# Seven-product MLP weights: product 4 is split from product 6's raw tile after GpSimd adds a block onto it in SBUF

## The chip, the cores and the metric

The kernel runs on 1 core of one Trainium2 chip. The metric is device microseconds for one execution of the whole program. Before the change the median of three runs is 756.41 us (756.36 to 757.88).

## The reference, cut to what matters

One layer of an encoder trunk, float32 in and out, 512 tokens, width 1024, hidden width 4096:

```python
h = h + jnp.concatenate([fox_out, rec], axis=-1) @ w_out[l]
h = h + memory_cross_attention(rmsnorm(h, norm_x_g[l]), mem_n, w_xq[l], w_xkv[l], w_xo[l])
u = rmsnorm(h, norm_ff_g[l]) @ w1[l]
h = h + jnp.square(jax.nn.relu(u)) @ w2[l]
return rmsnorm(h, final_norm_g)
```

The change is in the last two products, with `w1` (1024 x 4096) and `w2` (4096 x 1024).

## The kernel before, in words

Every weight is used as a sum of two parts, `hi` and `lo`. A raw float32 tile of 128 x 1024 is loaded into SBUF; ScalarE writes `hi` from it (line 181, tiles `wh...`), VectorE writes `lo = raw - hi` (line 185, tiles `wl...`); TensorE then runs three matmuls for each product of tiles: hi x hi, hi x lo, lo x hi.

The MLP is cut into eight sets `g` of 512 hidden columns. For each set there is an up part (with `w1`) and a down part (with `w2`). Up parts of sets 2 to 7 and all down parts use a seven-product scheme for 2 x 2 blocks: instead of eight block products there are seven, called 1, 5, 6, 2, 7, 3, 4 and run in this order. Products 1, 2, 3 use a block of the weights as it is; 5, 7, 6 and 4 use sums of blocks: W5 = W00 + W01, W7 = W01 + W11, W6 = W11 + W5, W4 = W10 + W6.

Those four sums are made in DRAM ahead of time (`sum_jobs`, line 430 on). For each, SyncE starts a copy of a block into a DRAM tile `ws...` (line 434), and GpSimd later starts an accumulating DMA that adds the second addend to it (line 444). So 14 weight sets (eight down, six up) make 56 copies and 56 accumulating DMAs. `Presum` spreads the 56 over the program: a counter of matmul work (`tick`) is compared with `PACE`, pairs of a start and a gap, and each accumulating DMA is made to wait for the matmul at which it fell due. `COPIES` says how many copies go out beside each load of the earlier stages.

A unit is one weight tile of one product. `load` starts the DMA of its raw tile on SyncE's queue (line 1328), up to `LOADS` = 8 units ahead of use; `prep` emits the two splits, up to 4 units ahead, since the pools of `wh` and `wl` tiles have four buffers. Tile names are made of kind, set and product: `whu36` is the hi part for up, set 3, product 6; `wrd24` is the raw tile for down, set 2, product 4.

In the up part (`mlp_up7`) the seven products share three PSUM banks. Products 1, 6, 7 and 4 accumulate in bank U, 5 and 3 in Y, 2 in V. Behind product 6 ScalarE copies U into Y (line 1411, tile `uY`):

```python
            elif name == "6":
                ac.activation(bank["Y"], ps, AF.Copy)
```

Product 2 runs in V meanwhile; product 7 writes U again and therefore waits for that copy. TensorE's order is written by hand; ScalarE's, VectorE's, GpSimd's and SyncE's orders come from a scheduler, and each of these engines runs its own list strictly in order. An instruction that waits holds up all that stand behind it on its engine.

Of the kernel before, what the change touches and what calls it, by code (L numbers as in the profile page):

```python
# [13 lines left out]
ALU = mybir.AluOpType  # L14
# [3 lines left out]
S = 512  # L18
# [4 lines left out]
WT = 256  # L23
# [14 lines left out]
X1, X2, X3, X4 = 1.5, 2.0, 1.5, 2.0  # L38
NEG = -3.0e38
SEVEN = (2, 3, 4, 5, 6, 7)  # L40
RAWS, HB, LOADS = 6, 4, 8
COPIES = {7: 2, 16: 1, 17: 0, 21: 1, 29: 2}
PACE = (183.0, 4.6), (306.0, 6.0), (385.0, 9.0)


@with_exitstack
def emit(
# [21 lines left out]
    nc = tc.nc  # L69
    te, ve, ac, gp = nc.tensor, nc.vector, nc.scalar, nc.gpsimd  # L70
# [26 lines left out]
    def s4(shape, name, dt=F32):  # L97
        return s4p.tile([P] + shape, dt, tag="s4", name=name)
# [7 lines left out]
    def t4(name):  # L106
        return t4p.tile([P, D], F32, tag="t4", name=name)

    def t2(name, dt=F32, shape=(S,)):
        return t2p.tile([P] + list(shape), dt, tag="t2", name=name)  # L110
# [18 lines left out]
    def f(a):  # L129
        return a.bitcast(F32)  # L130
# [39 lines left out]
    UW, UK = WT + FH, KC // 2  # L170

    def new_parts(shape, name):
        pad = [P, UK * (UW + FH)]
        hi = whp.tile([P, shape[0] * shape[1]], R, tag="wh", name=f"wh{name}", padded_shape=pad)
        lo = wlp.tile([P, shape[0] * shape[1]], R, tag="wl", name=f"wl{name}", padded_shape=pad)
        return [t.rearrange("p (k n) -> p k n", k=shape[0]) for t in (hi, lo)]

    def split_of(hi, lo, raw):
        def split(what="hl"):
            if "h" in what:  # L180
                ac.activation(hi, raw, AF.Copy)  # L181
            if "v" in what:
                ve.tensor_copy(hi, raw)
            if "l" in what:
                ve.tensor_tensor(lo, raw, f(hi), ALU.subtract)  # L185

        return split

    def load_unit(name, spec, ks, parts=1, between=None):
# [12 lines left out]
        for q in range(parts):  # L202
# [3 lines left out]
            if between is not None:  # L206
                between(q)
            for _ in range(next((n for at, n in reversed(COPIES.items()) if len(stream) >= at), 0)):
                if copies:
# [78 lines left out]
    def ahead(n):  # L288

        return tc.high_priority(offset=n) if n else nullcontext()  # L290

    class Fill:
        def __init__(self):
            self.q = deque()
            self.credit = 0.0
# [115 lines left out]
    hn_hi, hn_lo = act_tile("hn_hi"), act_tile("hn_lo")  # L411
    xTd = drp.tile([4, P, 2, S], F32, name="xTd")

    SUMS = {"5": ("00", "01"), "7": ("01", "11"), "6": ("11", "5"), "4": ("10", "6")}

    def block1(g, rc):
        r, c = int(rc[0]), int(rc[1])
        n0 = g * HG + c * WT
        return w1[r * S : (r + 1) * S, n0 : n0 + WT].rearrange("(k p) n -> p k n", p=P)

    def block2(g, rc):
        r, c = int(rc[0]), int(rc[1])
        k0 = g * HG + r * 2 * P
        return w2[k0 : k0 + 2 * P, c * S : (c + 1) * S].rearrange("(k p) n -> p k n", p=P)

    wsum = {}

    def sum_jobs(kind, g):
        block, shape = (block1, [P, UK, WT]) if kind == "u" else (block2, [P, 2, S])
        for name in SUMS:  # L430
            wsum[kind, g, name] = drp.tile(shape, F32, name=f"ws{kind}{g}{name}")

        def first(name):
            dma = nc.sync.dma_start(wsum[kind, g, name], block(g, SUMS[name][0]))
            copied.add((kind, g, name))
            return dma

        def sums():
            for name, (_, b) in SUMS.items():
                while (kind, g, name) not in copied:  # L440
                    copies.popleft()()
                src = wsum[kind, g, b] if b in SUMS else block(g, b)
                more = {"max_dma_last_dim": 2048} if b in SUMS else {}
                yield gp.dma_start(wsum[kind, g, name], src, accum_op=ALU.add, **more)  # L444

        return [lambda name=name: first(name) for name in SUMS], sums()

    class Presum:
        def __init__(self):
            self.jobs, self.spent, self.next, self.at = deque(), 0.0, PACE[0][0], None  # L450

# [12 lines left out]
        def tick(self, us, at):  # L464
            self.spent, self.at = self.spent + us, at
            while self.jobs and self.spent >= self.next:
                gap = next(gap for begin, gap in reversed(PACE) if self.next >= begin)
                if gap is None:
                    self.next = min(begin for begin, _ in PACE if begin > self.next)
                    continue  # L470
# [448 lines left out]
    for c in range(NT):  # L919
# [24 lines left out]
        with ahead(P1):  # L944
            hs = sm(4, f"hs{c}")
            for h in range(4):
                j = t2(f"hj{c}{h}", F32, (P,))
# [134 lines left out]
    for n in range(len(pairs) + 2):  # L1082
        if n < len(pairs):
            p, tb = pairs[n]
# [217 lines left out]
    for i in range(2):  # L1302
        gp.dma_start(gfin[i], final_norm_g[i * S : (i + 1) * S].partition_broadcast(P))
    HS = S // 2
    units, unit_q = {}, deque()
    sqs, comb, hbs = {}, {}, {}
    PRODUCTS = ("1", "5", "6", "2", "7", "3", "4")
    QUAD = {"1": "00", "2": "10", "3": "11"}
    raw_n = [0]

    def raw_tile(name):
        raw_n[0] += 1
        if raw_n[0] % RAWS == 4:
            return t4(f"wr{name}")
        if raw_n[0] % RAWS in (0, 2):
            return wrp.tile([P, D], F32, tag="wr", name=f"wr{name}", padded_shape=[P, UK * UW])
        return s4([D], f"wr{name}")

    load_q = deque()

    def add_unit(key, shape, src):

        name = "".join(map(str, key))
        box = []

        def load():
            raw = raw_tile(name).rearrange("p (k n) -> p k n", k=shape[0])
            nc.sync.dma_start(raw, src())
            box.append(raw)

        def prep():
            while not box:
                load_q.popleft()()
            unit = new_parts(shape, name)
            with ahead(PW):
                split_of(unit[0], unit[1], box[0])()
            units[key] = unit

        unit_q.append((key, prep))
        load_q.append(load)  # L1340

    def up_units(g):
        if g in SEVEN:
            for name in PRODUCTS:
                add_unit(("u", g, name), [UK, WT], lambda name=name: block1(g, QUAD[name]) if name in QUAD else wsum["u", g, name])
            return
        for j in range(2):
            for n in range(2):
                add_unit(("u", g, j, n), [UK, WT], lambda j=j, n=n: block1(g, f"{n}{j}"))

    def down_units(gs):
        for name in PRODUCTS:
            for g in gs:
                add_unit(("d", g, name), [2, S], lambda g=g, name=name: block2(g, QUAD[name]) if name in QUAD else wsum["d", g, name])

    def unit(*key):

# [278 lines left out]
    for g in range(NG):  # L1636
        if g >= 2:
            up_units(g)
        if 1 <= g < NG - 1:
            down_units((g - 1,))  # L1640
    down_units((NG - 2, NG - 1))
    order = [k for k, _ in unit_q]
    xsum = {}
# [78 lines left out]
```

## Time and profile before

| what | value |
|---|---|
| median of 3 runs | 756.41 us |
| the profiled execution's own time | 756.48 us |
| span of its trace, first to last instruction | 754.5 us |
| VectorE busy / ScalarE busy / GpSimd busy | 71% / 57% / 25% |
| DMA moved over the span | 162.85 MB, mean 216 GB/s |
| TensorE clock granted over the span | 0.999 |
| seven-product stage | about 450 to 748 us of the span |

Times in the trace count from the span's first instruction. A row of the timeline gives the start, how long, the engine, the line, the operation and its tiles, and in brackets how long the engine stood idle before it and what released it. A row of DMA issues gives the median from the issue to the landing of the last byte. Tile names stand there without set and product numbers.

### The profile page before, as it was taken

How to read it: one execution, taken by the hardware profiler on the slowest of the kernel's cores; microseconds unless marked ns; L12 is line 12 of the kernel's file. 1: busy time of each engine (PE TensorE's matmuls, PEld its weight loads, DVE VectorE, ACT ScalarE, POOL GpSimd, SP SyncE). 2: the span in 40 equal slices, each digit the busy share in tenths (PEclk: the TensorE clock that was granted, in tenths of full speed). 3: DMA queues.
4: the chain of work that ended last, by engine and by line, in shares of the span. 5: the costliest groups of instructions: out<-in, count | busy, mean ns of one | idle time of the engine just before them, and what ended most of it. 6: DMA issues, size and time to landing. Idle time of an engine off the chain costs nothing.

```text
span 754.5 us, 12053 instructions
## 1 busy us (share of the span) xinstructions
PE 746.1 (99%) x4501; PEld 648.9 (86%) x4501; DVE 537.4 (71%) x844; ACT 431.1 (57%) x715; POOL 190.3 (25%) x274
## 2 busy tenths in 40 slices
PE   9999999999999999999999999999999999999996
PEld 6889888888888988888888888898989899999985
DVE  5647873677878756745546558978787887879697
ACT  5655555655756532334434396657575757574873
POOL 7207531333342237620121211111000111000014
PEclk9999999999999999999999999999999999999999
DMA  8641987567947899996668879898979797977332
GB/s 251 196 117 57 310 262 226 177 225 252 312 165 222 264 280 290 287 245 128 140 151 182 179 127 312 198 314 229 296 186 298 190 281 205 265 220 248 121 112 112
DMA packets 112444, 162.85 MB, mean 216 GB/s; under 512 B 6482, under 2 KB 73595, under 8 KB 112387
## 3 DMA queue, kind: packets, MB, share of 16 engines
q1 hardware_dynamic: 91186, 123.80, 49.9%
q0 software_dynamic: 20608, 37.25, 27.2%
q10 hardware_dynamic: 592, 1.05, 0.4%
q8 instruction: 35, 0.57, 0.3%
q14 instruction: 23, 0.18, 0.1%
HBM read 157.87 MB, written 62.93 MB: 293 GB/s over the span
## 4 chain that ended last, share of the span: by engine, by line
PE 95%; DVE 1%; ACT 1%; POOL 1%; issue 1%; ACTq 0%; POOLq 0%
PE U L1528 4%; PE U L1527 4%; PE U L1529 4%; PE uU L1402 3%; PE uU L1401 3%; PE uU L1400 3%; PE xq L253 2%; PE wo L253 2%; PE xq L254 2%; PE xw L253 2%; PE xq L255 2%; PE xw L255 2%; PE u L255 2%; PE xw L254 2%; PE wo L255 2%; PE u L254 2%
## 5 line engine op out<-in xcount | busy, mean ns | idle before, releaser
L185 DVE TENSOR_TENSOR wld<-wrd,whd 128x1024 fp32r<-128x1024 f32 x56 | 69.6, 1244 | 17.4 <-ACT whd L181 17.3
L181 ACT ACTIVATE whd<-wrd 128x1024 fp32r<-128x1024 f32 x56 | 59.2, 1057 | 24.6 <-PE uV L1401 8.0
L181 ACT ACTIVATE whu<-wru 128x1024 fp32r<-128x1024 f32 x42 | 44.5, 1059 | 44.9 <-PE uU L1401 18.2
L185 DVE TENSOR_TENSOR wlu<-wru,whu 128x1024 fp32r<-128x1024 f32 x42 | 50.4, 1223 | 14.5 <-ACT whu L181 14.4
L1527 PE MATMUL U<-whd,hb 128*128 128x512 f32 x120 | 46.8, 390 | 0.0
L1528 PE MATMUL U<-wld,hb 128*128 128x512 f32 x120 | 46.8, 390 | 0.0
L1529 PE MATMUL U<-whd,hb 128*128 128x512 f32 x120 | 46.7, 389 | 0.0
L444 POOL DMA_DIRECT2D wsd<-in_w_dram x16 | 16.8, 1050 | 91.5 <-PE U L1529 27.9
L444 POOL DMA_DIRECT2D wsd<-wsd x16 | 14.3, 894 | 98.4 <-PE uU L1402 18.0
L1012 POOL TENSOR_SCALAR bi<-nF,Ft 128x128 f32<-128x128 f32 (+3 forms) x32 | 20.7, 656 | 60.2 <-PE pt L1044 34.7
L444 POOL DMA_DIRECT2D wsu<-in_w_dram x12 | 14.1, 1176 | 58.8 <-PE xq L255 11.4
L1155 ACT ACTIVATE x_hi<-hT,gv 128x512 fp32r<-128x512 f32 x16 | 11.5, 717 | 27.7 <-DVE hT L1154 27.7
L1402 PE MATMUL uU<-x_hi,wlu 128*128 128x256 f32 x96 | 27.2, 283 | 0.0
L1400 PE MATMUL uY<-xs_hi,whu 128*128 128x256 f32 x96 | 27.2, 283 | 0.0
L1401 PE MATMUL uY<-xs_lo,whu 128*128 128x256 f32 x96 | 27.2, 283 | 0.0
L1402 PE MATMUL uY<-xs_hi,wlu 128*128 128x256 f32 x96 | 27.2, 283 | 0.0
L1400 PE MATMUL uU<-xs_hi,whu 128*128 128x256 f32 x96 | 27.2, 283 | 0.0
L1401 PE MATMUL uU<-xs_lo,whu 128*128 128x256 f32 x96 | 27.2, 283 | 0.0
L1402 PE MATMUL uU<-xs_hi,wlu 128*128 128x256 f32 x96 | 27.2, 283 | 0.0
L1401 PE MATMUL uU<-x_lo,whu 128*128 128x256 f32 x96 | 27.2, 283 | 0.0
L1400 PE MATMUL uU<-x_hi,whu 128*128 128x256 f32 x96 | 27.1, 283 | 0.0
L1529 PEld LDWEIGHTS U<-whd,hb 128*128 128x128 f32 x120 | 22.5, 188 | 4.7
(995 smaller groups left out, 2655.2 us busy)
## 6 DMA issues: line engine op xcount, KB each, us to landing
wsd<-in_w_dram SPq DMA_DIRECT2D x32, 512.0 KB, 5.7
wrd<-wsd SPq DMA_DIRECT2D x32, 512.0 KB, 6.3
wsu<-in_w_dram SPq DMA_DIRECT2D x24, 512.0 KB, 7.1
wrd<-in_w_dram SPq DMA_DIRECT2D x24, 512.0 KB, 6.2
wru<-wsu SPq DMA_DIRECT2D x24, 512.0 KB, 6.2
wru<-in_w_dram SPq DMA_DIRECT2D x18, 512.0 KB, 5.8
wsd<-in_w_dram POOLq DMA_DIRECT2D x16, 512.0 KB, 8.0
wsd<-wsd POOLq DMA_DIRECT2D x16, 512.0 KB, 6.8
```

Of the source, the lines that this page charges most:

```text
L181: ac.activation(hi, raw, AF.Copy)
L185: ve.tensor_tensor(lo, raw, f(hi), ALU.subtract)
L253: te.matmul(ps, wh, hi, start=n_ == 0 and not begun, stop=False)
L254: te.matmul(ps, wh, lo, start=False, stop=False)
L255: at = te.matmul(ps, wl, hi, start=False, stop=k == order[-1])
L444: yield gp.dma_start(wsum[kind, g, name], src, accum_op=ALU.add, **more)
L1400: te.matmul(ps[:, i, :], whi[:, k, ws], xh[:, k, :], start=begin, stop=False, skip_group_check=True)
L1401: te.matmul(ps[:, i, :], whi[:, k, ws], xl[:, k, :], start=False, stop=False, skip_group_check=True)
L1402: at = te.matmul(ps[:, i, :], wlo[:, k, ws], xh[:, k, :], start=False, stop=k == UK - 1, skip_group_check=True)
L1527: te.matmul(ps, hi, whi[:, k, :], start=begin, stop=False, skip_group_check=True)
L1528: te.matmul(ps, hi, wlo[:, k, :], start=False, stop=False, skip_group_check=True)
L1529: at = te.matmul(ps, lo, whi[:, k, :], start=False, stop=k == 1, skip_group_check=True)
```

## The change

The sum W4 is no longer made in DRAM: `SUMS` loses "4", and with it 14 copies (SyncE), 14 accumulating DMAs from one DRAM tile to another (GpSimd) and 14 loads (SyncE) go. In their place product 6's raw tile is kept. Once both of its splits have read it, GpSimd starts an accumulating DMA that adds the block W10 from DRAM onto that tile in SBUF, and the two splits of product 4 read the same tile. The raw tiles of product 6 now always come from the pool `s4` (12 buffers) and are held until product 4 is split; `RAWS` goes from 6 to 5, so that the other raw tiles rotate over fewer places. `PACE` spreads the 42 sums that are left; `COPIES` loses its last entry.

```diff
-RAWS, HB, LOADS = 6, 4, 8
-COPIES = {7: 2, 16: 1, 17: 0, 21: 1, 29: 2}
-PACE = (183.0, 4.6), (306.0, 6.0), (385.0, 9.0)
+RAWS, HB, LOADS = 5, 4, 8
+COPIES = {7: 2, 16: 1, 17: 0, 21: 1}
+PACE = (183.0, 5.1), (306.0, 12.5)
...
-    SUMS = {"5": ("00", "01"), "7": ("01", "11"), "6": ("11", "5"), "4": ("10", "6")}
+    SUMS = {"5": ("00", "01"), "7": ("01", "11"), "6": ("11", "5")}
...
-        if raw_n[0] % RAWS == 4:
+        if raw_n[0] % RAWS == 3:
             return t4(f"wr{name}")
...
         def load():
-            raw = raw_tile(name).rearrange("p (k n) -> p k n", k=shape[0])
-            nc.sync.dma_start(raw, src())
+            if part == "4":
+                box.append(raws.pop((kind, g)))
+                return
+            if part == "6":
+                raw = raws[kind, g] = s4(shape, f"wr{name}")
+            else:
+                raw = raw_tile(name).rearrange("p (k n) -> p k n", k=shape[0])
+            if part in SUMS:
+                src = wsum[kind, g, part]
+            else:
+                src = block(g, QUAD[part] if part in QUAD else f"{key[3]}{part}")
+            nc.sync.dma_start(raw, src)
             box.append(raw)
...
             with ahead(PW):
                 split_of(unit[0], unit[1], box[0])()
+            if part == "6":
+                gp.dma_start(box[0], block(g, "10"), accum_op=ALU.add)
             units[key] = unit
```

TensorE's list of matmuls is the same in both kernels, matmul for matmul. Two places on the other engines matter below. The first is ScalarE's list in the up part of set 3. Before:

```order
L181 ACTIVATE whu36_5522<-wru36_5433 128x1024
L181 ACTIVATE whu32_5548<-wru32_5456 128x1024
L181 ACTIVATE whu37_5582<-wru37_5479 128x1024
L1406 ACTIVATE uV3_5579<-uU3_5547 128x512
L1476 ACTIVATE hb22_5711<-sq21_5137 128x512
L181 ACTIVATE whu33_5614<-wru33_5503 128x1024
L1409 ACTIVATE y53_5612<-uY3_5581 128x512
L181 ACTIVATE whu34_5645<-wru34_5526 128x1024
L1411 ACTIVATE uY3_5581<-uU3_5547 128x512
L181 ACTIVATE whd21_5677<-wrd21_5552 128x1024
```

And now:

```order
L181 ACTIVATE whu36_5482<-wru36_5393 128x1024
L181 ACTIVATE whu32_5507<-wru32_5416 128x1024
L181 ACTIVATE whu37_5540<-wru37_5439 128x1024
L1415 ACTIVATE uV3_5537<-uU3_5506 128x512
L181 ACTIVATE whu33_5572<-wru33_5462 128x1024
L1418 ACTIVATE y53_5570<-uY3_5539 128x512
L1485 ACTIVATE hb22_5669<-sq21_5100 128x512
L181 ACTIVATE whu34_5603<-wru36_5393 128x1024
L1420 ACTIVATE uY3_5539<-uU3_5506 128x512
L181 ACTIVATE whd21_5636<-wrd21_5511 128x1024
```

The split `whu34` reads `wru36`, the raw tile that `whu36` read seven rows above, in place of a raw tile of its own; `hb22` moved down by two rows; the copy `uY3` stands right behind `whu34`, as it did.

The second place is GpSimd's list near the end of the sums, before:

```order
L444 DMA wsd67_242<-in_w2_dram 256x1x512
L444 DMA wsd77_246<-in_w2_dram 256x1x512
L444 DMA wsd66_243<-wsd65_241 256x512
L444 DMA wsd76_247<-wsd75_245 256x512
L444 DMA wsd64_244<-wsd66_243 256x512
L444 DMA wsd74_248<-wsd76_247 256x512
```

And now:

```order
L444 DMA wsd67_230<-in_w2_dram 256x1x512
L1350 DMA wru56_6202<-in_w1_dram 128x4x256
L444 DMA wsd77_233<-in_w2_dram 256x1x512
L1350 DMA wrd46_6386<-in_w2_dram 128x2x512
L444 DMA wsd66_231<-wsd65_229 256x512
L444 DMA wsd76_234<-wsd75_232 256x512
L1350 DMA wru66_6607<-in_w1_dram 128x4x256
L1350 DMA wrd56_6791<-in_w2_dram 128x2x512
```

The two sums of W4 (`wsd64`, `wsd74`) are gone, and the additions onto raw tiles (`wru56`, `wrd46`, `wru66`, `wrd56`) stand between the sums that are left: `wru56` right behind `wsd67`, `wru66` right behind `wsd76`.

More of the change, by code (lines that the diff above doesn't have):

```diff
@@ L1304, in emit @@
     HS = S // 2
-    units, unit_q = {}, deque()
+    units, raws, unit_q = {}, {}, deque()
     sqs, comb, hbs = {}, {}, {}
@@ L1319, in emit, with add_unit @@
     load_q = deque()
-    def add_unit(key, shape, src):
+    def add_unit(key, shape):
+        kind, g, part = key[:3]
         name = "".join(map(str, key))
+        block = block1 if kind == "u" else block2
         box = []
         def load():
-            raw = raw_tile(name).rearrange("p (k n) -> p k n", k=shape[0])
-            nc.sync.dma_start(raw, src())
+            if part == "4":
[10 more added lines that the diff above has]
+            nc.sync.dma_start(raw, src)
             box.append(raw)
@@ L1342, in up_units @@
     def up_units(g):
[L1343 to L1349, printed above, removed]
+        for part in PRODUCTS if g in SEVEN else [(j, n) for j in range(2) for n in range(2)]:
+            add_unit(("u", g, part) if g in SEVEN else ("u", g, *part), [UK, WT])
     def down_units(gs):
@@ L1353, in down_units @@
             for g in gs:
-                add_unit(("d", g, name), [2, S], lambda g=g, name=name: block2(g, QUAD[name]) if name in QUAD else wsum["d", g, name])
+                add_unit(("d", g, name), [2, S])
     def unit(*key):
```

## The prediction

> **What bounds the kernel now.** First the page: the span, the engines' busy time, and the chain that ended last.
>
> ```profile
> span 754.5 us, 12053 instructions
> PE 746.1 (99%) x4501; PEld 648.9 (86%) x4501; DVE 537.4 (71%) x844; ACT 431.1 (57%) x715; POOL 190.3 (25%) x274
> ...
> PE 95%; DVE 1%; ACT 1%; POOL 1%; issue 1%; ACTq 0%; POOLq 0%
> ```
>
> TensorE fills the span. Busy could still hide waits, so I asked the view of waits for TensorE alone. It has two rows:
>
> ```profile
> PE warm L365 <- DVE ones L369: 1.3, 1, 1.3
> PE pt L1044 <- DVE bi L1036: 0.7, 1, 0.7
> ```
>
> 2.0 us, neither in the MLP. The table of windows (busy time and, in brackets, instructions of PE, PEld, DVE, ACT, POOL; then granted clock, DMA share, GB/s) has TensorE full over the whole stage:
>
> ```profile
> 440.00:690.00 250.00, 250.00 (x1501) 224.29 (x1501) 203.48 (x245) 165.42 (x223) 26.93 (x30) 1.00 0.89 240
> ```
>
> So nothing that goes off DMA, GpSimd or SyncE can shorten the path; the matmuls are the same. What the change can do is make TensorE wait where it doesn't today. I looked for the instruction at which it would, in the timeline of up set 3 (the names of set and product are from the engines' lists):
>
> ```profile
> 535.02 3.50 DVE L185 TENSOR_TENSOR wlu<-wru,whu 128x1024 fp32r<-128x1024 f32 x3
> ...
> 541.47 1.06 ACT L181 ACTIVATE whu<-wru 128x1024 fp32r<-128x1024 f32 x1 [1.34 <-PE uU L1401]
> 542.44 0.58 ACT L1411 ACTIVATE uY<-uU 128x512 f32<-128x512 f32 x1
> ...
> 542.57 1.23 DVE L185 TENSOR_TENSOR wlu<-wru,whu 128x1024 fp32r<-128x1024 f32 x1 [1.66 <-ACT whu L181]
> ...
> 544.27 0.28 PE L1400 MATMUL uU<-xs_hi,whu 128*128 128x256 f32 x1
> ```
>
> The first row is three lo splits, products 6, 2 and 7; a split takes 1.22, so product 6's ends at 535.02 + 1.22 = 536.24, the last reader of raw tile 6. At 541.47 ScalarE splits product 4, then copies U into Y until 542.44 + 0.58 = 543.02. At 544.27 product 7 writes U, which waits for that copy. Today the copy is 1.25 us early.
>
> **The change part by part.** *Removed:* 14 copies, 14 sums, 14 loads. All run beside a TensorE that never waits for them: 0 us. *RAWS, COPIES, the order of loads:* raw tiles are asked for some 20 us ahead and split when a `wh` buffer comes free, not when they land; the copies and sums left start no later than they need to. 0 us; the cover is that lead.
>
> *Added:* an accumulating DMA between product 6's lo split and product 4's hi split. Split 4 stands ahead of the copy uY on ScalarE, so a late landing delays the copy, and product 7 behind it. From 536.24 to 544.27 there are 8.03 us. The split and copy take 543.02 - 541.47 = 1.55. Each hand-over between engines takes about 0.04 (lo split 4 starts at 542.57, its hi split ends at 542.53), four of them 0.16. That leaves **6.3 us** from GpSimd's issue to the landing; each microsecond over it is lost by TensorE. It waits for nothing else there, and the next cycle keeps the spacing, so losses add up over the up sets.
>
> How long does such a DMA take? The view of DMA issues over the stage 440 to 690 us, where the last row is from the whole span:
>
> ```profile
> q0 software_dynamic: 8684, 14.72, 36.4%
> ...
> wsd<-wsd POOLq DMA_DIRECT2D x9, 512.0 KB, 6.9
> wsd<-in_w_dram POOLq DMA_DIRECT2D x8, 512.0 KB, 8.0
> wsu<-wsu POOLq DMA_DIRECT2D x6, 512.0 KB, 7.5
> wsu<-in_w_dram POOLq DMA_DIRECT2D x4, 512.0 KB, 7.7
> ```
>
> ```profile
> mt<-in_mem_dram POOLq DMA_DIRECT2D x2, 512.0 KB, 4.6
> ```
>
> No row adds onto SBUF. The nearest is the last but one, the same source, size and engine with a DRAM target: 7.7. The lower end is mt, a plain GpSimd load into SBUF: 4.6. For the upper end, five of today's sums start within 1 us of such a lo split's end in sets 2 to 6:
>
> ```profile
> 496.88 0.89 POOL L444 DMA_DIRECT2D wsu<-wsu  x1 [6.06 <-PE uU L1402]
> ...
> 654.48 0.88 POOL L444 DMA_DIRECT2D wsd<-wsd  x1 [8.14 <-PE uY L1402]
> ```
>
> Asked for one by one (issues at 496.88, 536.10, 575.32, 615.25, 654.48) they landed after:
>
> ```profile
> wsu<-wsu POOLq DMA_DIRECT2D x1, 512.0 KB, 9.8
> ```
>
> ```profile
> wsd<-in_w_dram POOLq DMA_DIRECT2D x1, 512.0 KB, 9.1
> ```
>
> ```profile
> wsd<-wsd POOLq DMA_DIRECT2D x1, 512.0 KB, 6.8
> ```
>
> ```profile
> wsd<-in_w_dram POOLq DMA_DIRECT2D x1, 512.0 KB, 7.8
> ```
>
> ```profile
> wsd<-wsd POOLq DMA_DIRECT2D x1, 512.0 KB, 8.7
> ```
>
> Upper end 9.8, median 8.7. It is a crowded moment: the next parts' loads are in flight, as the DMA share, the number before the last, shows for sets 3, 6 and 7.
>
> ```profile
> 536.20:542.70 6.50, 6.50 (x56) 6.50 (x55) 4.28 (x6) 4.46 (x7) 0.94 (x1) 1.00 1.04 300
> ...
> 653.90:660.40 6.50, 6.50 (x57) 6.50 (x56) 4.28 (x6) 4.47 (x7) 0.88 (x1) 1.00 1.03 330
> 692.50:699.60 7.10, 7.10 (x62) 7.10 (x61) 3.76 (x5) 4.34 (x6) 0.00 (x0) 1.00 0.79 267
> ```
>
> I take **7.4**: 7.7 less a tenth of the way to mt, for the target in SBUF. Sets 2 to 6 then lose 7.4 - 6.3 = 1.1 each, 5.5 in all.
>
> The Trainium skill speaks against this: its page "DMA: Bandwidth & Descriptors", section "Anatomy of one DMA — SWDGE (gpsimd) path", gives 2.0 us plus bytes / 436 GB/s, by which 512 KB would land after an estimated 3.2 us; the rows (6.8 to 9.8) don't agree. By it this term would be 0.
>
> *Queued behind another sum.* All GpSimd DMAs share queue 0. In the stage its 27 issues took 36.4% of 250 us, 91 us: 3.4 us of all 16 engines each. One that follows another closer than that I count as landing 3.4 behind it. Where are the sums? In today's timeline the last sum starts at 664.55 and the sixteenth from last at 516.90; fifteen gaps of 9.0 on the counter, 135.0, took 147.65, 1.094 us per unit:
>
> ```profile
> 516.90 1.05 POOL L444 DMA_DIRECT2D wsd<-in_w_dram  x1 [4.79 <-PE U L1529]
> ...
> 664.55 0.88 POOL L444 DMA_DIRECT2D wsd<-wsd  x1 [9.20 <-PE uU L1402]
> ```
>
> Today's last falls due at 520.2 on the counter; the new pace puts its last, wsd76, at 510.5, so 664.3 - 9.7 x 1.094 = 653.7, and wsd67, three gaps of 12.5 earlier, at 612.7. The lo splits of product 6 in sets 5 and 6:
>
> ```profile
> 613.46 3.50 DVE L185 TENSOR_TENSOR wlu<-wru,whu 128x1024 fp32r<-128x1024 f32 x3
> ...
> 652.68 3.50 DVE L185 TENSOR_TENSOR wlu<-wru,whu 128x1024 fp32r<-128x1024 f32 x3
> ```
>
> They end at 614.68 and 653.90. In set 5 the addition follows wsd67 by 2.1: +1.3. In set 6 it must wait for wsd76's issue (0.9, from 653.9 to 654.8: +0.9) and follows by 0.9: +2.5. Together **4.7**.
>
> *Set 7* has no sums beside it and a wider gap:
>
> ```profile
> 691.30 2.35 DVE L185 TENSOR_TENSOR wlu<-wru,whu 128x1024 fp32r<-128x1024 f32 x2
> ...
> 701.15 0.28 PE L1400 MATMUL uU<-xs_hi,whu 128*128 128x256 f32 x1
> ```
>
> 701.15 - 692.52 = 8.63, so 6.9 are allowed; at a DMA share of 0.79 I count 0, at 8.7 it would be 1.8.
>
> *Down sets.* Lo split 6 ends at 551.21 + 1.23 = 552.44, hi split 4 starts at 561.30; 8.8 are allowed, and no PSUM copy stands right behind it. 0.
>
> ```profile
> 551.21 1.23 DVE L185 TENSOR_TENSOR wld<-wrd,whd 128x1024 fp32r<-128x1024 f32 x1 [0.28 <-ACT whd L181]
> ...
> 561.30 1.06 ACT L181 ACTIVATE whd<-wrd 128x1024 fp32r<-128x1024 f32 x1
> ```
>
> **Sum:** 5.5 + 4.7 = 10.2 on the span of 754.5; outside the span the profiled execution has 2.0 (756.48), which stays. 756.48 + 10.2 = 766.7, and against the median, 756.41, I say 766.5.
>
> **The rivals.** *It lands in time* (the other side). If the addition onto SBUF is more like mt than like the sums, below 6.3 us, the copy uY is never late in sets 2 to 5, and where queue 0 interleaves its DMAs not in 6 either. For it: DRAM is neither read nor written for the target. Against it: the DMA share of 1.04 in the very window. Time 756.5. It decides at 6.3; between 4.6 and 6.3 with strict queueing, set 6 alone loses up to 3.4 and set 5 up to 1.3, 758 to 761.
>
> *All land late.* The five same-phase sums are the measure: 8.7 - 6.3 = 2.4 in five sets, 12.0, 4.7 for the queue and 1.8 in set 7: 18.5, time 775.
>
> *The clock drops in the longest hole.* Set 6's hole is 1.1 + 3.4 = 4.5 us. If an idle TensorE gets a slower clock, it pays again afterwards. No hole of such length is in this trace; 0 by its rows, granted clock 1.00 in the windows above. The Trainium skill's "TensorE: Matmul & The Clock Gate", section "Part 1: The HAM clock gate (the "warmup" mystery)", has half the clock after an idle window of some 3.4 us, until a busy window as long; an estimate by it is 1.7 us more, 768; no run here shows it.
>
> *Raw tiles come late.* Tile 6 is held over four units more, so loads could find no place, and `wh` splits would starve at TensorE. Against it: a lead of 20 us. Price at one missed load per cycle of about 3 us, six cycles: 785.
>
> *Less DMA early shortens the first 440 us.* The most there is to win is the two waits, 2.0 us: 754.5.
>
> **How the numbers follow.** Forecast (a late uY in up sets, 758 to 772) 0.65; all late 0.13; in time 0.13; clock 0.03; raw tiles 0.02; early gain 0.04. A measurement of this kernel tells 0.2%, 1.5 us, from none. Faster 0.04; same 0.13; slower 0.83. The range reaches from "in time" to "all late": 756.5 to 775; left out are the early gain, the late raw tiles and the outer halves of those two.
>
> **What would show it.** TensorE's waits get rows for the first matmul of product 7 (uU) released by ScalarE's uY, six of them at most, the longest in set 6; ScalarE's split whu gets waits for a DMA in front of them; a row wru<-in_w_dram on POOLq near 7.4 us. In the down sets no TensorE wait. I am wrong if that row is under 6.3, if waits of TensorE name a `wh` or `wl` tile, or if time moves before 440 us.

## The result and the profile after

The changed kernel takes 789.32 us (median of 6 runs, 787.72 to 792.20), the kernel before 756.41 on the same chip (755.73 to 757.88): a ratio of 1.0437 (95% interval 1.0413 to 1.0462). The sign was forecast, the size was not: 33 us were lost in place of 10. Below, a time that is set against a trace is that execution's own span: 754.5 before, 786.2 after.

The page of the changed kernel: the span, TensorE's row (busy time, share of the span, instructions), and the chain that ended last by engine and by line.

```profile
span 786.2 us, 11996 instructions
...
PE 755.5 (96%) x4501; PEld 656.6 (84%) x4501; DVE 541.3 (69%) x844; ACT 430.4 (55%) x715; POOL 196.5 (25%) x274
...
PE 66%; issue 21%; DMA 5%; POOL 3%; DVE 2%; ACT 2%; SPq 0%; POOLq 0%; ACTq 0%; DVEq 0%
```

TensorE has gone from 99% to 96%, and DMA, which had no share of the chain, has 5%. (The 21% under "issue" are not idle TensorE: here the chain is followed back along GpSimd's list, and what lies between two of its DMAs is counted there, 13.03 us behind the sum at 503.71 for example.) But TensorE's busy time has grown too, from 746.1 to 755.5, with the same 4501 matmuls: 9.4 us that no wait explains. So there are two losses to look for. The view of waits for TensorE (total, how many, longest; a fourth row, 0.3 us, is left out), and one row of the same view for ScalarE:

```profile
PE uU L1409 <- ACT uY L1420: 21.8, 6, 5.0
PE warm L365 <- DVE ones L369: 1.3, 1, 1.3
PE pt L1044 <- DVE bi L1036: 0.7, 1, 0.7
```

```profile
ACT whu L181 <- DMA wru<-in_w_dram: 35.4, 6, 7.2
```

This is the place that was forecast: six waits of product 7 (uU) on the copy uY, and one step back six waits of ScalarE's split whu on the addition. Up set 3 shows the chain in the timeline, ScalarE first, then TensorE:

```profile
544.34 0.62 ACT L1485 ACTIVATE hb<-sq 128x512 fp32r<-128x512 f32 x1
549.99 1.06 ACT L181 ACTIVATE whu<-wru 128x1024 fp32r<-128x1024 f32 x1 [5.03 <-DMA wru<-in_w_dram]
550.95 0.58 ACT L1420 ACTIVATE uY<-uU 128x512 f32<-128x512 f32 x1
```

```profile
551.59 0.39 PE L1409 MATMUL uU<-xs_hi,whu 128*128 128x256 f32 x1 [2.85 <-ACT uY L1420]
```

ScalarE stands idle for 5.03 us in front of the late split; the copy, which itself needs nothing that is late, stands behind it; TensorE has a hole, a stretch without work, of 2.85 us. The holes of sets 2 to 7 are 2.2, 2.9, 4.3, 5.0, 4.9 and 2.5. Against the matmuls of before, no shift worth naming arises ahead of 440 us or in a down set.

How late the additions onto a raw tile land, from the view of DMA issues (KB, then median from issue to landing): first over 440 to 760 us, then the six up additions one by one, sets 2 to 7.

```profile
wrd<-in_w_dram POOLq DMA_DIRECT2D x8, 512.0 KB, 5.8
...
wru<-in_w_dram POOLq DMA_DIRECT2D x6, 512.0 KB, 9.8
```

```profile
wru<-in_w_dram POOLq DMA_DIRECT2D x1, 512.0 KB, 8.9
...
wru<-in_w_dram POOLq DMA_DIRECT2D x1, 512.0 KB, 8.2
...
wru<-in_w_dram POOLq DMA_DIRECT2D x1, 512.0 KB, 10.5
...
wru<-in_w_dram POOLq DMA_DIRECT2D x1, 512.0 KB, 11.2
...
wru<-in_w_dram POOLq DMA_DIRECT2D x1, 512.0 KB, 11.0
...
wru<-in_w_dram POOLq DMA_DIRECT2D x1, 512.0 KB, 9.1
```

The same 512 KB onto SBUF take 5.6 to 6.4 us in down sets 0 to 5 (7.3 and 10.0 in sets 6 and 7, where the second follows the first by 2.3 us) and 8.2 to 11.2 in an up set. Two things differ: the hour, and the packets, 256 of 2 KB in a down set and 512 of 1 KB in an up set. The windows during up set 3's addition, down set 2's, down set 4's and up set 7's (busy time and instructions of five engines, then granted clock, DMA share, GB/s):

```profile
541.70:549.90 8.20, 7.03 (x59) 6.83 (x57) 2.94 (x3) 2.06 (x3) 2.50 (x2) 1.00 1.03 286
560.10:565.80 5.70, 5.70 (x29) 4.74 (x28) 3.90 (x6) 4.17 (x6) 1.20 (x1) 1.00 0.67 127
...
652.50:658.90 6.40, 6.40 (x32) 5.33 (x31) 4.61 (x7) 4.69 (x7) 1.21 (x1) 1.00 1.00 234
721.90:731.00 9.10, 8.27 (x69) 8.06 (x68) 3.05 (x3) 2.64 (x4) 1.30 (x1) 1.00 0.98 244
```

The DMA share alone does not tell them apart: down set 4's addition took 6.4 us beside a share of 1.00. By the packet records SyncE's queue started 0.2 MB of loads while down set 2's addition was in flight, 0.8 beside down set 4's, and 1.3 to 2.1 beside the six up additions. e5, e6 and e7 below take queue, packets and loads one at a time.

The second loss is in the column of the granted clock, the share of full speed at which TensorE was allowed to run. Windows cut where that column changes, around the holes of sets 2 and 3, and then of set 4 (in the second fence the last row comes first in time):

```profile
505.94:509.35 3.41, 1.56 (x13) 1.57 (x14) 1.83 (x2) 3.13 (x5) 0.00 (x0) 1.00 1.01 199
509.35:512.76 3.41, 3.41 (x19) 3.41 (x18) 1.99 (x3) 2.03 (x3) 0.00 (x0) 0.50 0.56 156
546.90:550.31 3.41, 1.83 (x16) 1.63 (x14) 0.00 (x0) 0.32 (x1) 1.17 (x1) 1.00 1.06 249
550.31:553.72 3.41, 2.13 (x17) 2.14 (x18) 2.40 (x2) 3.31 (x5) 0.00 (x0) 1.00 1.13 160
553.72:557.14 3.42, 3.42 (x31) 3.42 (x30) 2.54 (x4) 2.96 (x4) 0.00 (x0) 1.00 0.54 162
```

```profile
594.68:598.09 3.41, 2.77 (x13) 2.77 (x14) 2.45 (x2) 3.23 (x6) 0.00 (x0) 0.50 0.22 47
598.09:601.50 3.41, 3.41 (x18) 3.41 (x18) 1.34 (x2) 0.94 (x2) 1.08 (x1) 0.50 0.62 140
...
591.27:594.68 3.41, 0.00 (x0) 0.00 (x0) 0.00 (x0) 0.95 (x1) 0.00 (x0) 1.00 0.59 181
```

A matmul here has 256 columns; an interval of 3.41 us filled with them has 18 or 19 at 0.50 and 31 at 1.00. Set 4's hole empties a whole interval, and two intervals at half follow; set 2's leaves 1.56 of 3.41 busy, and one follows; set 3's, though longer than set 2's, is cut in two by the border at 550.31, and none follows. In all, 20.5 us of the MLP run at half, TensorE busy in 18.2 of them.

What each loss is worth follows from the start of every matmul in the two traces. The changed kernel is 0.35 us behind ahead of the first hole, falls back at the six holes by 2.4, 3.0, 4.4, 5.2, 5.1 and 2.7, together 22.8 (0.16 more than each wait), and in between by 1.6, 0.1, 2.8, 1.6 and 2.4, together 8.4. The 0.1 of set 3, where no half clock follows, is lost at the second matmul behind the hole; the rest arises where the clock is at half. 0.35 + 22.8 + 8.4 = 31.5 of the 31.7 us by which the spans differ.

### The profile page after: what moved, and what is told of

It is laid out like the page before. It is cut to its first block, busy times and chain, and to the rows that moved or that the text cites. A ratio compares the mean times of both kernels' runs of the same rounds, so it can differ in the third digit from the quotient of the medians.

```text
span 786.2 us, 11996 instructions
## 1 busy us (share of the span) xinstructions
PE 755.5 (96%) x4501; PEld 656.6 (84%) x4501; DVE 541.3 (69%) x844; ACT 430.4 (55%) x715; POOL 196.5 (25%) x274
## 4 chain that ended last, share of the span: by engine, by line
PE 66%; issue 21%; DMA 5%; POOL 3%; DVE 2%; ACT 2%; SPq 0%; POOLq 0%; ACTq 0%; DVEq 0%
DMA wru<-in_w_dram 4%; PE wo L253 2%; PE xw L255 2%; PE xw L254 2%; PE xw L253 2%; PE u L253 2%; PE wo L254 2%; PE u L254 2%; PE u L255 2%; PE wo L255 2%; PE xq L254 2%; PE xq L255 2%; PE xq L253 2%; PE U L1537 1%; PE pv L1060 1%
## 5 line engine op out<-in xcount | busy, mean ns | idle before, releaser
L1409 PE MATMUL uU<-xs_hi,whu 128*128 128x256 f32 x96 | 31.3, 326 | 21.8 <-ACT uY L1420 21.8
L1409 PEld LDWEIGHTS uU<-xs_hi,whu 128*128 128x128 f32 x96 | 21.7, 226 | 23.0 <-ACT uY L1420 23.0
L1350 POOL DMA_DIRECT2D wrd<-in_w_dram x8 | 9.6, 1198 | 93.6 <-DVE wld L185 93.6
L1410 PE MATMUL uU<-xs_lo,whu 128*128 128x256 f32 x96 | 30.5, 317 | 0.0
L1411 PE MATMUL uU<-xs_hi,wlu 128*128 128x256 f32 x96 | 30.4, 317 | 0.0
```

The costliest lines, as they stand in the source:

```text
L1409: te.matmul(ps[:, i, :], whi[:, k, ws], xh[:, k, :], start=begin, stop=False, skip_group_check=True)
L1410: te.matmul(ps[:, i, :], whi[:, k, ws], xl[:, k, :], start=False, stop=False, skip_group_check=True)
L1411: at = te.matmul(ps[:, i, :], wlo[:, k, ws], xh[:, k, :], start=False, stop=k == UK - 1, skip_group_check=True)
```

## The experiments

The edits are made on the changed kernel. All but e3, e8, e11 and e12 are a single execution, beside before at 756.5 to 756.7. Executions of the changed kernel itself lie between 787.7 and 796.5 (e9), so a single time a few us apart decides little; waits, landings and clock in the trace do. "Landings" are those of the six up additions, sets 2 to 7.

**e1: is it what stands behind the late split?** The hi split of product 4 is put behind the copy uY on ScalarE.

```diff
-                ac.activation(hi, raw, AF.Copy)
+                made = ac.activation(hi, raw, AF.Copy)
+                if behind is not None:
+                    order_only = mybir.DependencyInfo(mybir.DependencyClass.NoSync, mybir.DependencyReason.DATA)
+                    tc.add_manual_dep(made.ins, behind.ins.name, order_only, reason="behind")
...
-                split_of(unit[0], unit[1], box[0])()
+                split_of(unit[0], unit[1], box[0])(behind=ycopy.get(g) if (kind, part) == ("u", "4") else None)
...
-                ac.activation(bank["Y"], ps, AF.Copy)
+                ycopy[g] = ac.activation(bank["Y"], ps, AF.Copy)
```

> The changed kernel, with product 4's hi split in the up parts placed one row lower on ScalarE, behind the copy uY. Theory (TensorE waits for uY because that split, which waits for the addition's landing, stands ahead of it): the six waits of uU on uY go, 21.8 us and the 10 us lost to the halved clock with them. The next late thing is then VectorE's sum sq (uU with y5), which product 4 waits for and which stands behind lo split 4, lo split d1 and an hb part: the landing + 5.6 us. Landings after 8.2 to 11.2 us make that some 8 us in sets 2 to 6, so 764 to 768, and no dip of the clock. Rival (the additions slow TensorE through DMA or SBUF traffic, or raw tiles come late): still 780 to 790.

Measured 775.96. The waits on uY are gone, and the next thing late is the one that was named, VectorE's sum sq, which stands behind product 4's lo split:

```profile
PE uU L1412 <- DVE sq L1427: 13.9, 6, 5.4
```

The place is confirmed; the time missed its range by 8, since landings (9.8, 8.3, 11.2, 9.9, 13.3, 9.6) and half clock (10.2 us of it, none expected) were both underrated again.

**e2: do holes or traffic drop the clock?** TensorE gets 20 matmuls on a spare bank ahead of product 7, so that it works through most of the hole.

```diff
+NFILL = 20
...
+            if name == "7":
+                junk = sc(f"junk{g}").rearrange("p (i n) -> p i n", i=2)
+                for n in range(NFILL):
+                    te.matmul(junk[:, 0, :], whi[:, n % UK, 0:P], xh[:, n % UK, :], start=n == 0, stop=n == NFILL - 1, skip_group_check=True)
```

> The changed kernel, with 20 filler matmuls of 256 columns into a spare PSUM bank ahead of product 7 in each up part of sets 2 to 7 (2.4 us each where the clock is full). They add nothing to the output. Theory (the trace has 21.8 us of holes, and about 10 us more because the granted clock halves after a hole): fillers run inside the holes, what is left of the waits for uY is about 8 us with none over 3 us, the clock stays at 1.0, and the time falls by about 10 us although 120 matmuls are added: 777 to 781. Rival (the slower matmuls behind the holes come from the addition's traffic, not from the idle time): the slow matmuls stay, 787 to 792.

Measured 785.58, above the theory's 781 and below the rival's 787. The holes that are left are at most 4.1 us, and half clock fell from 20.5 us to 3.4, one interval behind the longest, at a traffic that was no smaller (60.82 MB over 440 to 760 us, 60.80 in the changed kernel). So holes drop the clock, and the traffic does not. The time missed because in sets 2 to 6 the additions, issued at the same place, landed later still (9.5 to 12.6; 7.9 in set 7), so that fillers and holes together, 14.4 + 11.7 us, are more than the 21.8 us of holes that they replace.

```profile
PE uU L1414 <- ACT uY L1425: 11.7, 5, 4.1
```

**e3 and e4: down sets alone, up sets alone.** `names_of(kind)` keeps the old sum W4 for the other kind; the gap of `PACE` is set so that the sums end where the change has them.

```diff
+    def names_of(kind):
+        return [n for n in SUMS if n != "4" or kind != KEPT]
...
-            if part == "6":
+            if part == "6" and kind == KEPT:
                 gp.dma_start(box[0], block(g, "10"), accum_op=ALU.add)
```

> Only the eight down parts keep the change; in the up parts W4 is summed in DRAM and loaded as before (48 sums, gap 8.5 in place of 12.5 so that the last one falls at about the same time). Theory (all of the loss sits in the up parts): 756.0 to 757.5, no wait of TensorE in the MLP, GpSimd's additions onto wrd landing after 5.5 to 9 us. Rival (holding raw tile 6, five raw places or GpSimd's queue cost something by themselves): 759 or more.

> Only the six up parts keep the change; in the down parts W4 is summed in DRAM and loaded as before (50 sums, gap 8.0). Theory: the loss of the changed kernel is all here, 784 to 795; with more sums and more loads beside them the additions land after 8 to 12 us, and the clock dips in sets where the hole is over about 4 us. Rival (the loss is shared): 765 to 780.

Down alone: 756.98 (10 runs), ratio 1.0002 (0.9989 to 1.0015), with no wait of TensorE in the MLP. Up alone: 791.14, as long as the changed kernel itself. The whole loss is in the up sets, and eight copies, sums and loads fewer gain nothing.

**e5: the queue.** All 42 sums are over before the first addition.

```diff
-PACE = (183.0, 5.1), (306.0, 12.5)
+PACE = ((183.0, 3.9),)
```

> Only the pace of the 42 sums in DRAM changes: they come every 3.9 on the counter, so that the last starts before the first addition onto a raw tile. GpSimd's queue then carries nothing but the additions in the MLP. After: the up additions land 8.9, 8.2, 10.5, 11.2, 11.0, 9.1 us after their issue in sets 2 to 7, with packets of other sums ahead in sets 4, 5 and 6. Theory (the queue makes sets 4 to 6 longer than the others, the crowd of SyncE's loads does the rest): sets 4 to 6 fall to 8.5 to 9.5, sets 2, 3 and 7 stay within 1 us; waits of uU on uY 14 to 18 us in place of 21.8; with the half clock after the longest hole or two 771 to 781 us. Rival 1 (the queue is all of it): all six land in 6.5 or less, no waits, 757. Rival 2 (the queue is nothing): 10 to 11 in sets 4 to 6 as before, waits 20 or more, 784 to 790.

Measured 776.73, the time as the theory had it; landings 8.4, 8.2, 8.2, 8.2, 7.9, 10.6. Sets 4 to 6 land 2.3 to 3.1 us earlier, somewhat more than expected, sets 2 and 3 0.5 and 0.0. Set 7, with no sums in either kernel, became 1.5 longer, which the theory did not have: by the packet records 1.9 MB of SyncE's loads were started while it was in flight, 1.0 to 1.3 in the others. That the loads are the cause is not shown by this run alone.

```profile
PE uU L1409 <- ACT uY L1420: 13.9, 6, 3.8
```

```profile
wru<-in_w_dram POOLq DMA_DIRECT2D x6, 512.0 KB, 8.2
```

**e6: the cut of the packets.** An up block's rows are 1 KB in DRAM, a down block's 2 KB. W10 of the up sets is copied to DRAM tiles with 4 KB together, and added from there.

```diff
+WIDTH = 2048
...
+            more = [lambda: nc.sync.dma_start(w10[g], block(g, "10"))]
...
-                gp.dma_start(box[0], block(g, "10"), accum_op=ALU.add)
+                if kind == "u":
+                    gp.dma_start(box[0], w10[g], accum_op=ALU.add, max_dma_last_dim=WIDTH)
+                else:
+                    gp.dma_start(box[0], block(g, "10"), accum_op=ALU.add)
```

> W10 of the six up sets is first copied by SyncE, early, into a DRAM tile in which each partition's 4 KB lie together, and the addition reads it from there in pieces of 2 KB in place of 1 KB; bytes, place in the order and sums stay. Theory (an up addition lands late since its 512 packets of 1 KB take turns with the loads' packets, where the quiet down additions have 256 of 2 KB): the up additions land 1.5 to 3 us earlier, 6.5 to 8.5; waits of uU on uY 6 to 13 us in place of 21.8; 760 to 775 us. Rival (the bytes that are in flight set the time, whatever their cutting): landings 8 to 11 as after, waits 20 or more, 782 to 792.

Measured 783.40; landings 9.0, 9.2, 8.9, 9.5, 10.0, 9.2, median 9.2; waits of 17.7 us, between what theory and rival had. Packets were 256 of 2 KB at a median of 176 ns in place of 512 of 1 KB at 102, and the median landing moved by 0.6: sets 4 to 6 are 1.1 to 1.7 earlier, 2, 3 and 7 are 0.1 to 1.0 later. The rival is nearer, and a gain from the cutting is not shown: in set 7, which has no sum beside it, the first packet started 1.9 us after the issue in place of 3.9, and yet the landing was the same (9.2 against 9.1).

```profile
wru<-w POOLq DMA_DIRECT2D x6, 512.0 KB, 9.2
```

**e7: the crowd**, that is, SyncE's loads beside the additions. In the MLP all of them, except those of product 6's tiles, bring half their bytes; the splits read that half twice, so that the other half of those weights is left out of the products.

```diff
+        whole = part in "64" if len(key) == 3 else True
...
-            nc.sync.dma_start(raw, src)
+            n = shape[0] if whole else shape[0] // 2
+            nc.sync.dma_start(raw[:, 0:n], src[:, 0:n])
...
+                    twice = box[0][:, 0:n].unsqueeze(1).to_broadcast([P, 2, n, shape[1]])
```

> In the MLP every load by SyncE except that of part 6 brings only half of its tile, and the split reads that half twice (the other half of those weight blocks is left out of the computation); the additions, the sums, every instruction of the engines and their sizes stay. Theory (SyncE's loads, 3.8 to 6.2 us of packets on each DMA engine while an up addition is in flight, make up the time above the quiet one): the up additions land about 2 to 3 us earlier, 6 to 8 in sets 2, 3 and 7, 7.5 to 9 in sets 4 to 6; waits of uU on uY 3 to 11 us in place of 21.8; 758 to 772. Rival (the crowd is nothing; the queue and the small packets are all): landings as after within 0.5, waits 20 or more, 783 to 790.

Measured 779.11; landings 7.7, 7.2, 8.9, 9.5, 10.3, 7.8. Every set is earlier, by 0.7 to 1.7 (1.2 on the mean), less than the theory's 2 to 3. The waits fell to 14.4 and not to 11 or less, and the time missed its range by 7.

```profile
PE uU L1416 <- ACT uY L1427: 14.4, 6, 4.2
```

**e10: both together.**

> The early sums of e5 and the half loads of e7 together (half of each MLP weight tile except those of parts 6 and 4 is left out of the computation). Theory (queue and crowd are separate terms: 2.7 us off the landings of sets 4 to 6 by the sums, 1.1 to 1.7 off all by half the loads): the up additions land after 6.8 to 7.5 us in all six sets, waits of uU on uY 4 to 8 us, at most two half-clock intervals, 759 to 766. Rival (the one hides behind the other, so that the second brings nothing more): landings about 8 as in e5, waits 12 or more, 770 to 777.

Early sums as in e5, half loads as in e7. Measured 765.72; landings 7.1 to 7.8, waits 7.1, no half clock. The terms add: the mean landing fell by 1.2 in e5, by 1.2 in e7 and here by 2.3. What is left over the 5.8 of the down sets was not taken apart by a run; 1.1 of it lies ahead of the first packet, which started 3.0 to 3.2 us after the issue of an up addition and 1.9 to 2.0 after that of a down addition (sets 1 to 5).

```profile
wru<-in_w_dram POOLq DMA_DIRECT2D x6, 512.0 KB, 7.6
```

**e9: the changed kernel again, for a rule of the clock** read off the seven traces before it.

> The changed kernel itself, a second time, for the clock. In the seven traces so far (of the changed kernel and e1, e2, e4 to e7) the half clock begins on a grid of 3.413 us, and of the grid's intervals those in which TensorE was idle for 1.85 us or more are followed by one at half clock, those with 1.79 or less are not; a second one at half follows where 0.65 us or more of the first is idle. Theory (that rule): every half interval of this trace answers to it, where the holes fall on the grid this time decides how many there are; each costs 1.7 us; 783 to 792 in all. Rival (the length of the hole decides, from 2.4 or 3 us up): holes of like length are treated alike, wherever they lie on the grid.

Measured 796.51, 4.5 above the range: waits of 25.7 us, and 30.7 us at half clock. The landings, 10.9, 8.5, 11.3, 10.5, 10.9 and 10.7, differ from the first trace's by up to 2.0 (set 2, later), with the same kernel. So a difference of 1 or 2 us in one set of one trace says little; of the comparisons above, the 2.3 to 3.1 of sets 4 to 6 in e5 (2.3 to 3.1 against this trace too) and the sign of e7 (0.6 to 3.1 earlier than here, in all sets) stand. All fourteen intervals with a part of a hole in them answer to the rule. Those of set 2 and set 3, with the interval behind, from the windows:

```profile
505.69:509.10 3.41, 0.77 (x7) 0.56 (x5) 0.00 (x0) 0.01 (x1) 0.00 (x0) 1.00 1.08 260
509.10:512.51 3.41, 1.82 (x8) 1.82 (x9) 2.10 (x2) 3.38 (x5) 0.00 (x0) 0.50 0.37 68
550.06:553.47 3.41, 2.38 (x20) 2.18 (x19) 0.00 (x0) 0.00 (x0) 1.17 (x1) 1.00 1.17 241
553.47:556.88 3.41, 1.24 (x10) 1.24 (x11) 1.51 (x2) 2.83 (x4) 0.00 (x0) 1.00 1.11 191
556.88:560.29 3.41, 3.41 (x18) 3.41 (x18) 1.74 (x3) 1.74 (x4) 0.00 (x0) 0.50 0.79 194
```

Set 3's hole of 3.2 us leaves 1.0 idle in one interval (the next is at full clock) and 2.2 in the other (the next is at half). The rival falls: a hole of 2.85 in the first trace of this kernel had cost no half interval, this one did, and one of 1.9 in e7 did; in e5 two holes of 1.96 stand in one trace, of which set 4's was followed by half clock and set 3's, cut by a border, was not.

**e8: is the addition harmless if nothing waits behind it?** Product 4's hi split is put behind product 7's square on ScalarE, its lo split between the sums of 7 and 3 on VectorE.

```diff
+            if ahead_[0] == "u" and ahead_[2:] == ("4",) and len(order) - len(unit_q) > at + 1:
+                break
...
+                low = split_of(unit[0], unit[1], box[0])(behind=after7.get(g) if (kind, part) == ("u", "4") else None)
...
-                square(qb[:, :, h2], qb[:, :, h2], -1.0)
+                after7[g] = square(qb[:, :, h2], qb[:, :, h2], -1.0)
...
-                ve.tensor_tensor(qb[:, :, h1], ps, y5, ALU.add)
+                stands_behind(ve.tensor_tensor(qb[:, :, h1], ps, y5, ALU.add), lo4[g])
```

> Nothing of the additions, sums or loads changes. In the six up sets product 4's splits are made after product 7 is through: the hi split stands on ScalarE behind product 7's square, the lo split on VectorE between product 7's sum and product 3's. The addition then has some 15 us to land in place of 6.3. Theory (the additions cost time only through what stands behind the late hi split): landings as after (8 to 12 us), no wait of TensorE for them, no hole, so no half clock: 756 to 757.5 us, level with before. Rival 1 (the traffic itself slows TensorE or its clock): no waits of TensorE, yet half clock and 762 or more. Rival 2 (the lateness moves on to the down set's first splits, which now stand behind product 4's): waits of TensorE on wh or wl tiles of the down sets, 760 to 775.

Measured 767.66, ratio 1.0149 (1.0132 to 1.0166): the time missed. But in the up parts no instruction of ScalarE waits for an addition any more, at landings of 9.0 to 11.4 (one down split does, for 1.6 us, and TensorE waits for nothing there), and the trace (765.71) has no half clock in the MLP. What TensorE waits for is the two splits, which I had put too late: in each set product 4 waits some 0.25 us for its hi part and 0.75 for its lo part. These twelve waits, 6.0 us, put the matmuls back by 9.1, as each loses 0.16 at its matmul and 0.1 at the next.

```profile
PE uU L1422 <- DVE wlu L191: 4.5, 6, 0.8
PE uU L1420 <- ACT whu L185: 1.5, 6, 0.3
```

**e11: the splits between the two places**, hi behind product 2's square, lo right behind product 7's sum. The cut is against e8.

```diff
+                stands_behind(low, add7[g])
...
-                square(ps, qa[:, :, h1])
+                after2[g] = square(ps, qa[:, :, h1])
...
-                ve.tensor_tensor(qb[:, :, h2], ps, y5, ALU.add)
-                after7[g] = square(qb[:, :, h2], qb[:, :, h2], -1.0)
+                add7[g] = ve.tensor_tensor(qb[:, :, h2], ps, y5, ALU.add)
+                square(qb[:, :, h2], qb[:, :, h2], -1.0)
```

> As e8, with product 4's splits between its two places: the hi split stands on ScalarE behind product 2's square (so behind the copy uY) and the lo split on VectorE right behind product 7's sum. In e8 the hi split stood behind product 7's square, ended 0.25 us after product 3 did, and the lo split 1.0 us later still; its trace has no wait of ScalarE for the additions, and the 1.4 to 1.5 us that each set lost are those two. Theory: the additions, landing 9 to 12 us after issue, are now hidden and the splits are 1 to 2 us earlier than in e8: no wait of TensorE in the up sets, no half clock, 756 to 757.5 us. Rival 1 (in the sets with the longest landings, 10.5 to 11.4 us, the addition itself is late for the lo split): waits of uU on DVE wlu or ACT whu in sets 5 and 6, 0.3 to 1.5 us each, 757 to 760. Rival 2 (the hi split now holds up the squares and the down splits behind it on ScalarE): waits on hb, wh or wl tiles of the down sets, 758 to 768.

Measured 762.33, ratio 1.0068 (1.0049 to 1.0087). Sets 2, 3 and 7 lose nothing; 4, 5 and 6, whose additions land after 11.6, 11.7 and 12.2, do: rival 1, at a higher price (its range ended at 760), since the two waits of set 6 also drew an interval at half.

```profile
PE uU L1423 <- DVE wlu L191: 1.8, 3, 0.8
PE uU L1421 <- ACT whu L185: 1.6, 2, 1.0
```

**e12: e11 with the early sums of e5.**

> The splits of product 4 where e11 has them, and the early sums of e5. In e11 sets 2, 3 and 7 (landings 9.2, 8.0, 9.5) lost nothing and sets 4, 5 and 6 (11.6, 11.7, 12.2, with other sums on the queue) lost 0.5 to 2 us each; from issue to product 4's first matmul, less the hi split of 1.06, there are 11.0 us. Theory (landing against that slack decides, and the sums are what puts sets 4 to 6 beyond it): landings 7.9 to 10.6 as in e5, no wait of TensorE in the up sets, 756 to 757.5 us, level with before and not below it, since TensorE is full. Rival 1 (the sums, paced 3.9, now cost in the part before 440 us): the same without waits, but 758 or more with the shift before 440 us. Rival 2 (landings in this order of splits are longer than in e5): waits as in e11, 759 to 763.

Measured 756.63 (11 runs) against 756.36, ratio 1.0002 (0.9993 to 1.0011): level, as the theory had it. The landings and all waits of TensorE that are left:

```profile
wru<-in_w_dram POOLq DMA_DIRECT2D x6, 512.0 KB, 8.2
```

```profile
PE warm L371 <- DVE ones L375: 1.3, 1, 1.3
PE pt L1050 <- DVE bi L1042: 0.7, 1, 0.7
```

The additions still take 8.2 us; with some 12 to land in (13.0 to 13.9 from the issue to product 4's first matmul, less the hi split of 1.06) and no sums on their queue they are free. With the 14 copies, sums and loads gone and nothing lost, the time is the one of before: TensorE was full, and there was nothing to gain.

## Why the prediction was right or wrong, point by point

**Where and how: right.** Product 7 waits for uY, uY stands behind the late split, the split waits for the addition; no wait names a `wh` or `wl` tile; nothing moves before 440 us. e1, e8 and e11 show it by moving what stands behind.

**Removed work and raw tiles at 0: right** (e3, e12), though the loads of before started 11 to 18 us ahead of their splits in the trace, and not 20. **Down sets at 0: right**: 5.6 to 6.4 us of the 8.8 allowed in sets 0 to 5; in 6 and 7 (7.3 and 10.0) no instruction of TensorE waited either.

**The 6.3 us allowed: right, for five sets.** A landing less its hole gives 6.1 to 6.6 in sets 2 and 4 to 7, and 5.3 in set 3, where GpSimd's issue started 1.2 us after the lo split's end and not 0.3 to 0.55 as elsewhere; why is open. I had counted the issue as immediate.

**The landing, taken at 7.4: mis-sized.** This is the first step that failed. With no sum on the queue the median is 8.2 (e5), with the sums and loads as they are 9.8. The mistake was the choice between the ends. The five sums of before that started at the same moment of the cycle gave 6.8 to 9.8, median 8.7, which is the mean of what sets 2, 3 and 7 then measured (8.9, 8.2, 9.1: 8.7). I took a median over all hours of the stage in their place, and even shortened it for a target in SBUF, of which no run shows a sign. The base term was 5.5 for five sets and 0 for set 7; it came to 13.5 for six, that is, 21.8 less the 8.3 of the next point (e5 as a whole has 13.9). Set 7 was put at 0 for a DMA share of 0.79, which came from before, where that stretch was not the same: during set 7's addition the changed kernel's share is 0.98, by the same view, and down set 4's 6.4 us at a share of 1.00 show that the share is no measure of the landing.

**The queue, 4.7 in sets 5 and 6: mis-sized.** In e5 the holes of sets 4 to 6 are 2.3, 3.0 and 3.0 us shorter, together 8.3. The two sums stood where I had put them (2.6 and 0.6 us ahead of the additions, for 2.1 and 0.9). But I let a sum weigh only as far as it started within 3.4 us ahead; yet of the one issued 4.7 us ahead of set 4's addition 138 of 256 packets started behind the addition's issue, and in sets 5 and 6 all 256.

Together the holes are 21.8 in place of 10.2. That is near the rival "all late", whose 18.5 was built on those same-phase rows; it had a chance of 0.13.

**The clock, put at 0 in the sum (chance 0.03, one interval): the term that was missing.** I asked only whether the longest hole, 4.5 us in set 6, might pay, and set it to 0 since the trace of before had "no hole of such length". It has one: TensorE's last matmul ends 6.3 us before the span does, and the clock is at half behind the first idle interval.

```profile
749.78:753.20 3.42, 0.00 (x0) 0.00 (x0) 0.83 (x2) 0.72 (x1) 0.05 (x1) 1.00 0.82 307
753.20:754.47 1.27, 0.00 (x0) 0.00 (x0) 0.00 (x0) 0.00 (x0) 0.00 (x0) 0.50 0.00 0
```

The runs show that the length of a hole is not what counts. In these traces the clock changes only on a grid of 3.413 us. In eleven traces of this kernel and its variants, all 29 full-clock intervals of the MLP with 1.85 us or more of TensorE idle were followed by one at half, none of the 57 with 0.3 to 1.70; between them, one of 1.79 was not, one of 1.72 (e11) was. So a hole of 1.9 us (set 3 of e7) can cost an interval at half, 1.6 us, and one of 2.85 across a border nothing; where holes fall on the grid changes from run to run. With six holes of 2 to 5 us this was no rival but a term: 8.4 us here and, worked out in the same way, some 12 in e9, where the holes were also 4 us longer; the two make all but 0.9 of the 8.5 us by which the two traces of this kernel differ.

The Trainium skill's page "TensorE: Matmul & The Clock Gate", section "Part 1: The HAM clock gate (the "warmup" mystery)", has a free-running window of 3413 ns, and the grid agrees with it; it has half the clock after an idle window, and here half an idle window was enough. The Trainium skill's page "DMA: Bandwidth & Descriptors", section "Anatomy of one DMA — SWDGE (gpsimd) path", by which the prediction gave an estimate of 3.2 us for 512 KB, disagrees with all additions seen: 5.8 in the quiet, 8.2 to 11.2 in the crowd.

## What to carry to other kernels

Before a DMA is put between two steps, read how long one like it takes at that very moment of the cycle, with its queue and its neighbours, not a median over the stage; and look at what else stands behind the instruction that will wait for it, since here only that paid. Where an engine is full, taking traffic away gains nothing, and a hole torn into it can cost more than its length: count the clock with every hole of some 2 us. The tail of the trace, where an engine has run out of work, can show what idle time does to its clock before anything is changed. The cheap repair is order: let the waiting instruction stand as late as its own user allows (e11), and keep other work off its queue in those stretches (e12).

## What the hardware showed that was not expected

- Half clock follows where TensorE was busy for less than about half of one 3.413 us interval (1.56 of 3.41 busy: half; 1.83: full). A second interval at half follows where the first was itself idle for 0.64 us or more (nine times), and none where it was idle for 0.55 or less (0.41 and 0.55 in two, and those without a hole).
- An addition of 512 KB onto SBUF takes 5.7 us where hardly any other DMA runs (down set 2) and 7 to 13 in the crowd of an up set (7.1 in e10, 13.3 in e1). A sum ahead of it on the same queue adds 2.3 to 3.1, half of SyncE's loads 1.2 on the mean of six sets. The same kernel's landings differ by up to 2.0 us between two traces, and nothing here says why.
- A hole costs 0.16 us more than its wait at the matmul that waited (six shifts of 22.8 for waits of 21.8 here, 8.1 for 7.1 in e10) and 0.1 more at the next one, so that many short waits are dear: 6.0 us of them cost 9.1 in e8.
